# Retrieval by gathered rows for 160 of 512 tokens instead of 128, with 72 expert blocks computed ahead instead of 48

## The chip, the cores and the metric

The kernel runs on one core of one Trainium2 chip. A core has TensorE (matrix products; PE in the profile), VectorE (DVE), ScalarE (ACT), GpSimd (POOL) and SyncE (SP), which here only starts transfers. Each engine works through its own queue in order and waits at semaphores for the others. The metric is the time of one execution on the device in microseconds (us), the median of several runs.

## The reference

One decoder layer on 512 tokens of width 1024 in float32: gated linear attention and sliding-window attention, merged into x, and then product-key retrieval of single-neuron experts (PEER), which the change is about:

```
def peer_layer(xn, w_pq, sub_keys, expert_u, expert_v):
    qp = (xt @ w_pq).reshape(t, 8, 2, 128)
    scores = jnp.einsum('thpd,hpkd->thpk', qp, sub_keys)
    s_top, i_top = lax.top_k(scores, 16)
    ...
    best, pos = lax.top_k(cand, 16)
    idx = jnp.take_along_axis(cand_idx, pos, axis=-1)
    gate = jax.nn.softmax(best, axis=-1)
    ...
        u = expert_u[ib]
        h = jax.nn.gelu(jnp.einsum('lkd,ld->lk', u, xb), approximate=False)
        return jnp.einsum('lk,lkd->ld', gb * h, expert_v[ib])
```

Each token chooses 8 x 16 = 128 of 16384 experts, and an expert is one row of U and one row of V, 1024 wide.

## The kernel before

Attention, merging and the queries of the retrieval come first (up to 660 us); the change leaves them almost alone. The retrieval then treats the tokens in two ways.

*Dense tokens.* For 384 tokens (TD) all experts are computed. There are 128 blocks of 128 experts. A **U block** (`h_step`) multiplies a block of U with the normalised tokens: 8 x 3 = 24 matmuls with a moving operand of TD columns, since each float32 is split into a high part (`whi`, made by ScalarE) and a low part (`wlo`, made by VectorE, by GpSimd for the first blocks) and three of the four products are kept. Gelu by ScalarE puts the result into a ring of SBUF tiles. A **V step** (`v_step`) weights it with the gates (`wr`, then its parts `wh` and `wl`) and multiplies with a block of V: 3 groups of 128 tokens x 3 products x 2 halves of 512 columns = 18 matmuls, summed in PSUM over all 128 blocks. The stream `st` loads and splits the weights two blocks ahead, with three tiles each for raw, `whi` and `wlo`.

*The gates* of the dense tokens are sparse, and are made dense by one-hot products: `decode` finds the expert numbers of 128 tokens on VectorE, TensorE transposes them (`ijp`, read by ScalarE into `ijg`), `onehot` makes two one-hot matrices for 4 tokens on VectorE, `gmm` multiplies them on TensorE (`gp`), ScalarE copies the product into `gbuild`, and after every 8 groups of 4 tokens ScalarE's queue writes 2 MB of gates to DRAM (`gd`). Later `gt` reads them back by block.

*Gathered tokens.* For the other 128 tokens (TG), one to a partition, GpSimd gathers by indirect transfer one row of U for each of the 128 chosen experts, and VectorE multiplies it with the token and sums (L1128); then 128 rows of V, which VectorE adds up with their weights (L1131). That is 256 steps of 128 x 1024.

*Order.* All is written out by hand. N0 = 48 U blocks run ahead. The ring holds NRING = 32 results; the blocks between 32 and 48 are spilled to DRAM (`hs<-hw`, L1154, from ScalarE's queue) and read back later (`hr`). Between the pieces of these blocks `feed` puts steps of the generator `route`: decoding and the one-hot groups. Then `dense_order` mixes: a V step, and behind it one of the remaining U blocks where a ring tile is free (a **pair**), else the V step alone. Gather steps begin at block 47 and are dealt out by a fixed count (`work(0.7)`, `work(1.5)`):

```
    for n, (kind, b) in enumerate(todo):
        if kind == "U":
            h_step(b)
            work(1.5)
            continue
        paired = n + 1 < len(todo) and todo[n + 1][0] == "U"
        h_load(b + WA + 2)
        w_a(b + WA)
        work(0.7 if paired else 0.4)
        w_b(b + WA)
        v_step(b)
        work(0.7 if paired else 0.4)
```

Rows are gathered four at a time into one of two buffers (`gbuf`): the next four are asked for when the first of the current four is used.

Of the kernel before, what the change touches and what calls it, by code (L numbers as in the profile page):

```python
# [20 lines left out]
D = 1024  # L21
# [13 lines left out]
RS = (4, 6, 7)  # L35
DS = (4, 6, 8, 11, 13, 15, 18, 23)
# [8 lines left out]
N0 = 48  # L45
NRING = 32
NOO = 6
AHEAD = 5
LEAD = 11
TAIL = 3  # L50
GL = 2
GS = 1
WA = 2
TG = 128
# [25 lines left out]
def tile_block(ctx, tc, xT, wst, smalls, wgk2, keysT, uT, vv, u_rows, v_rows, out):  # L80
# [736 lines left out]
    xtok = XP.tile([128, D], F32, name="xtok")  # L817
    x1s = DR.tile([128, NT, D], F32, name="x1s")
# [111 lines left out]
    for hp in range(17):  # L930
        if hp < 16:
# [26 lines left out]
        if hp in (5, 6):  # L958
            xtok_fill(hp - 5)
        if hp == 7:  # L960
            c16 = XP.tile([128, 16, 128], BF, name="c16", tag="xn0")
            clo = XP.tile([128, 16, 128], BF, name="clo")
            for c_, steps in ((c16, ((0, 16, 1, 0),)), (clo, LO)):
                for a0, na, st_, b0 in steps:
                    nc.gpsimd.iota(c_[:, a0:a0 + na], pattern=[[st_, na], [0, 128]], base=b0, channel_multiplier=0,
                                   allow_small_or_imprecise_dtypes=True)
        if hp:
            scores(hp - 1)
        if hp % 2 and hp >= 3:
            cands((hp - 3) // 2)  # L970
# [5 lines left out]
    eidx = XP.tile([128, 128], I32, name="eidx")  # L976
    wgt = XP.tile([128, 128], F32, name="wgt")
# [14 lines left out]
    def positions():  # L992
# [5 lines left out]
        nc.vector.scalar_tensor_tensor(q, pf, 48.0, i3, OP.is_ge, OP.add)  # L998
        nc.vector.scalar_tensor_tensor(q2, q, 0.5, i1, OP.mult, OP.add)
# [4 lines left out]
    def eq_mult(t, sd):  # L1004
        eq = R.tile([128, 16, 128], BF, name="eq", tag="eq", bufs=1)
        nc.vector.tensor_tensor(eq, pb[:, sd, t, None, :].to_broadcast([128, 16, 128]), c16 if sd else clo,
                                OP.is_equal if sd else OP.is_ge)
        e4 = eq.rearrange("p a (k h) -> p a k h", h=8)
# [4 lines left out]
    def decode(t):  # L1013
# [48 lines left out]
    def route():  # L1062
# [7 lines left out]
        nc.vector.tensor_copy(kh(pbf[:, 0]), posu.rearrange("p t h k -> p t k h"))  # L1070
        positions()
# [3 lines left out]
        nc.scalar.activation(b32, b32, AF.Exp)  # L1075
        yield
        d1 = decode(1)
        for _ in range(7):
            next(d1)
        ss = R.tile([128, 32], F32, name="gsum")  # L1080
        nc.vector.tensor_reduce(ss, b32, AX.X, OP.add)
        nc.vector.reciprocal(ss, ss)
        nc.vector.tensor_tensor(b32, b32, ss[:, :, None].to_broadcast([128, 32, 16]), OP.mult)
        yield
        next(d1, None)
        n = 32 * (NT - 1)
        for i in range(AHEAD):
            onehot(i)
        yield
        dec = None  # L1090
        for i in range(n):
            if i % 32 == DS[0]:
                dec = decode((i // 32 + 2) % NT)
            if dec is not None and i % 32 in DS:
# [6 lines left out]
    def gather():
# [232 lines left out]
```

## Time and profile before

| | |
|---|---|
| median of 3 runs | 1855.3 us (1854.67 to 1855.85) |
| the profiled execution, its own time | 1860.8 us |
| its span, first to last instruction | 1859.0 us |
| mean granted TensorE clock | 0.99 of full speed |
| busy | TensorE 1799.7 us, VectorE 1336.0, ScalarE 746.4, GpSimd 590.5 |
| moved by transfers | 387.14 MB |

Busy time is the time in which an engine has an instruction under way. Matmuls overlap in the engine's pipeline, so a row's duration is longer than the distance from one matmul to the next; how long a block takes is read from the starts in the chain. Of TensorE's clock the profile gives the share of full speed that was granted.

### The profile page before, as it was taken

How to read it: one execution, taken by the hardware profiler on the slowest of the kernel's cores; microseconds unless marked ns; L12 is line 12 of the kernel's file. 1: busy time of each engine (PE TensorE's matmuls, PEld its weight loads, DVE VectorE, ACT ScalarE, POOL GpSimd, SP SyncE). 2: the span in 40 equal slices, each digit the busy share in tenths (PEclk: the TensorE clock that was granted, in tenths of full speed). 3: DMA queues.
4: the chain of work that ended last, by engine and by line, in shares of the span. 5: the costliest groups of instructions: out<-in, count | busy, mean ns of one | idle time of the engine just before them, and what ended most of it. 6: DMA issues, size and time to landing. Idle time of an engine off the chain costs nothing.

```text
span 1859.0 us, 25029 instructions
## 1 busy us (share of the span) xinstructions
PE 1799.7 (97%) x9331; PEld 1568.1 (84%) x9331; DVE 1336.0 (72%) x2688; ACT 746.4 (40%) x1126; POOL 590.5 (32%) x433
## 2 busy tenths in 40 slices
PE   7999999999998998899999999999999999999998
PEld 5676688887887898899988898988899998988887
DVE  7657714355349988898867878777778888888764
ACT  4435523334253244566553333333333333333332
POOL 2433344444545530000013333331335343343100
PEclk9999999999999999899999999999999999999999
DMA  4221122222333233555788988998889999898753
GB/s 162 69 67 46 57 91 80 80 71 89 119 125 120 69 114 109 168 177 166 212 278 318 336 327 327 336 343 328 318 320 346 331 325 344 314 340 322 265 187 135
DMA packets 149018, 387.14 MB, mean 208 GB/s; under 512 B 11280, under 2 KB 64656, under 8 KB 148512
## 3 DMA queue, kind: packets, MB, share of 16 engines
q1 hardware_dynamic: 60368, 223.00, 33.8%
q0 software_dynamic: 36864, 134.23, 20.2%
q10 hardware_dynamic: 51664, 28.31, 5.4%
q8 instruction: 73, 1.20, 0.3%
q14 instruction: 49, 0.40, 0.1%
HBM read 353.00 MB, written 32.51 MB: 207 GB/s over the span
## 4 chain that ended last, share of the span: by engine, by line
PE 51%; DMA 1%; ACTq 1%; ACT 0%; DVE 0%; issue 0%; DVEq 0%
PE hp L179 21%; PE oacc L1194 10%; PE oa__8345 L1194 5%; PE oa__8346 L1194 5%; PE oa__8347 L1194 5%; PE oa__8348 L1194 5%; PE gp L1055 2%; DMA hs<-hw 1%; ACTq L1154 1%; ACT gbuild L1056 0%; ACT hw L1152 0%; ACT whi L129 0%; DVE wlo L130 0%; ACTq L1060 0%; DVE oh L1044 0%
## 5 line engine op out<-in xcount | busy, mean ns | idle before, releaser
L129 ACT CAST whi<-raw 128x1024 fp32r<-128x1024 f32 x349 | 365.0, 1047 | 226.2 <-issue 87.3
L130 DVE TENSOR_TENSOR wlo<-raw,whi 128x1024 fp32r<-128x1024 f32 x252 | 308.7, 1225 | 153.5 <-ACT whi L129 153.2
L179 PE MATMUL hp<-xh,whi 128*128 128x384 f32 x1024 | 354.3, 346 | 3.6 <-ACT hw L1152 3.6
L179 PE MATMUL hp<-xh,wlo 128*128 128x384 f32 x1024 | 345.8, 338 | 5.5 <-DVE wlo L130 5.5
L179 PE MATMUL hp<-xl,whi 128*128 128x384 f32 x1024 | 345.9, 338 | 0.0
L1108 POOL DMA_INDIRECT rows<-in_u_rows_dram,eidx x128 | 144.2, 1126 | 543.2 <-DVE oh L1044 277.5
L130 POOL TENSOR_TENSOR wlo<-raw,whi 128x1024 fp32r<-128x1024 f32 x97 | 239.8, 2476 | 237.0 <-ACT whi L129 236.2
L1108 POOL DMA_INDIRECT rows<-in_v_rows_dram,eidx x128 | 147.4, 1151 | 231.3 <-DVE acc L1131 184.2
L179 PEld LDWEIGHTS hp<-xh,whi 128*128 128x128 f32 x1024 | 194.4, 190 | 7.5 <-ACT hw L1152 3.9
L179 PEld LDWEIGHTS hp<-xh,wlo 128*128 128x128 f32 x1024 | 194.1, 190 | 6.2 <-DVE wlo L130 6.2
L179 PEld LDWEIGHTS hp<-xl,whi 128*128 128x128 f32 x1024 | 194.6, 190 | 3.4
L1152 ACT ACTIVATE ring<-hp 128x384 f32<-128x384 f32 x112 | 55.7, 497 | 313.8 <-PE hp L179 312.9
L1131 DVE SCALAR_TENSOR_TENSOR acc<-rows,wgt,acc 128x1024 f32<-128x1024 f32 x128 | 163.9, 1280 | 0.7
L1128 DVE SCALAR_TENSOR_TENSOR rows<-rows,xtok 128x1024 f32<-128x1024 f32 x128 | 154.7, 1220 | 0.0
L1056 ACT COPY gbuild<-gp 128x512 f32<-128x512 f32 x96 | 105.9, 1123 | 60.9 <-PE gp L1055 60.2
L1184 DVE TENSOR_TENSOR wl<-wr,wh 128x384 fp32r<-128x384 f32 x128 | 71.5, 558 | 71.8 <-ACT wh L1176 71.8
L1176 ACT CAST wh<-wr 128x384 fp32r<-128x384 f32 x128 | 65.3, 510 | 134.1 <-PE oa__8348 L1194 78.6
L179 PE MATMUL mm<-hhi,whi 128*128 128x512 f32 x264 | 108.0, 409 | 0.9 <-DVE gb L577 0.9
L1044 DVE TENSOR_SCALAR oh<-iof,ijg 128x128 f32<-128x128 f32 x384 | 107.1, 346 | 0.0
L1055 PE MATMUL gp<-oh 128*128 128x128 f32 x768 | 102.9, 278 | 1.6 <-ACT gbuild L1056 1.6
L179 PE MATMUL mm<-hhi,wlo 128*128 128x512 f32 x264 | 104.2, 395 | 0.0
L179 PE MATMUL mm<-hlo,whi 128*128 128x512 f32 x264 | 103.8, 393 | 0.0
(560 smaller groups left out, 3574.9 us busy)
## 6 DMA issues: line engine op xcount, KB each, us to landing
raw<-in_uT_dram SPq DMA_DIRECT2D x128, 512.0 KB, 5.1
raw<-in_vv_dram SPq DMA_DIRECT2D x128, 512.0 KB, 5.5
raw<-in_wst_dram SPq DMA_DIRECT2D x93, 512.0 KB, 3.4
gt<-gd SPq DMA_DIRECT2D x32, 768.0 KB, 6.5
gd<-gbuild ACTq DMA_DIRECT2D x11, 2048.0 KB, 10.7
hs<-hw ACTq DMA_DIRECT2D x16, 192.0 KB, 4.4
hr<-hs SPq DMA_DIRECT2D x16, 192.0 KB, 5.9
xt<-in_xT_dram SPq DMA_DIRECT2D x8, 256.0 KB, 6.6
```

The lines of the kernel that those rows point to most:

```text
L129: nc.scalar.copy(hi, r)
L130: self.lo_eng(u).tensor_tensor(lo, r, hi.bitcast(F32), OP.subtract)
L179: nc.tensor.matmul(ps[:, :n], a[:, kb, :], b[:, kb, c0:c0 + n], start=(kb == 0 and i == 0), stop=(kb == KB - 1 and i == 2))
L1044: nc.vector.tensor_scalar(o[:, 1, k], iof, ijg[:, 0, t0 + k:t0 + k + 1], ijg[:, 2, t0 + k:t0 + k + 1], OP.is_equal, OP.mult)
L1055: nc.tensor.matmul(p[:, k], o[:, 0, k], o[:, 1, k], start=True, stop=True)
L1056: nc.scalar.copy(gbs[c].rearrange("p i t -> p t i")[:, q * 4:q * 4 + 4, :], p)
L1108: nc.gpsimd.indirect_dma_start(out=b_[:, i], out_offset=None, in_=rows, in_offset=bass.IndirectOffsetOnAxis(ap=eidx[:, 4 * g + i:4 * g + i ...
L1128: nc.vector.scalar_tensor_tensor(cur[:, i], cur[:, i], 1.0, xtok, OP.mult, OP.mult, accum_out=hd[:, s_:s_ + 1])
L1131: nc.vector.scalar_tensor_tensor(acc, cur[:, i], wgt[:, s_:s_ + 1], acc, OP.mult, OP.add)
L1176: nc.scalar.copy(hi, wr)
L1184: nc.vector.tensor_tensor(lo, wr, hi.bitcast(F32), OP.subtract)
L1194: nc.tensor.matmul(accs[2 * t + hf], a[:, ts], v_[:, hf * 512:(hf + 1) * 512], start=(b == 0 and i == 0), stop=(b == NB - 1 and i == 2))
```

## The change

160 tokens are gathered, 352 computed densely. The 32 new gathered tokens lie on 128 partitions as four copies: copy r has the slots 32 r to 32 r + 31, so that 32 more gathers of U and 32 of V serve them (steps "x" and "y"), and a matmul with a 0/1 matrix (`sel`) adds the four partial sums at the end. A U block has 352 columns instead of 384; a V step has still 18 matmuls, with a first weight of 96 columns. There are 88 one-hot groups instead of 96. 72 blocks run ahead instead of 48, and the ring has 25 tiles instead of 32, so that 47 blocks are spilled instead of 16. The routing is cut into smaller steps, which stand after blocks 4 to 19 (`RS`) and then between pieces of blocks 20 to 66. Gather steps begin at block 19; they are dealt out by two running totals, `dve` and `pe`, to which the program adds a fixed number of microseconds for each piece of work that it issues: `pump` issues steps as long as VectorE's total is less than 3 us ahead of TensorE's. In the order 56 pairs and 72 lone V steps follow the first block of V (before: 80 and 48).

```diff
-RS = (4, 6, 7)
-DS = (4, 6, 8, 11, 13, 15, 18, 23)
+RS = (4, 7, 8, 10, 11, 11, 12, 13, 13, 14, 15, 16, 17, 18, 19)
+POOLLO = 8
+DS = {32: (4, 6, 8, 11, 13, 15, 18, 23), 24: (1, 3, 5, 7, 9, 11, 13, 16)}
...
-N0 = 48
-NRING = 32
+N0 = 72
+NRING = 25
...
-LEAD = 11
-TAIL = 3
+LEAD = 20
+TAIL = 5
+SLACK = 3.0
...
-TG = 128
+XG = 32
+XR = 128 // XG
+TG = 128 + XG
+TB = 128 - XG
...
-        nc.scalar.copy(xn0[:, kb], hr.pop(kb)[:, 0:TG])
+        h = hr.pop(kb)
+        nc.scalar.copy(xn0[:, kb, 0:128], h[:, 0:128])
+        nc.scalar.copy(xn0[:, kb, 128:].rearrange("p (r t) -> p r t", t=XG),
+                       h[:, None, 128:TG].to_broadcast([128, XR, XG]))
...
         if hp == NXU - 1:
+            for hf in range(4):
+                xtok_fill((xtok, xtk2)[hf // 2], hf // 2 * 128, hf % 2)
...
-        nc.vector.tensor_tensor(eq, pb[:, sd, t, None, :].to_broadcast([128, 16, 128]), c16 if sd else clo,
+        nc.vector.tensor_tensor(e4, pk[:, None].to_broadcast([128, 16, 16, 8]),
+                                (c16 if sd else clo)[:, :, None, :].to_broadcast([128, 16, 16, 8]),
                                 OP.is_equal if sd else OP.is_ge)
...
-        yield
         gk = R.tile([128, 128], F32, name="gkh", tag="gkh")
         nc.vector.tensor_copy(gk.rearrange("p (k h) -> p k h", h=8), gf)
+        if t == 1:
+            e1 = R.tile([128, 128], I32, name="e1")
+            nc.vector.scalar_tensor_tensor(e1, ij[:, 0], 128.0, ij[:, 1], OP.mult, OP.add)
+            for r in range(XR):
+                rs = slice(r * XG, (r + 1) * XG)
+                nc.sync.dma_start(eid2[rs, :], e1[0:XG, rs])
+                nc.sync.dma_start(wgt2[rs, :], gk[0:XG, rs])
+        yield
         p = PS.tile([128, 3, 128], F32, name="ijp", tag="PT")
...
+        steps = ([("u", s_) for s_ in range(128)] + [("x", s_) for s_ in range(XG)]
+                 + [("v", s_) for s_ in range(128)] + [("y", s_) for s_ in range(XG)])
...
+            while n < min(len(steps), k + (5 if late[0] else 4)):
+                for _ in range(4 if late[0] else 1):
...
+            dve[0] += (1.31 if kind in "vy" else 1.2) * (1.2 if late[0] else 1)
+            yield
...
-        for t in range(TD // 128):
-            ts = slice(t * 128, t * 128 + 128)
+        for t in range(3):
+            ts = slice(max(128 * t - XG, 0), 128 * t + 128 - XG)
...
+    def pump(slack):
+        while side and dve[0] < pe[0] + slack:
+            step()
...
+        if b == RS[0]:
+            dve[0] = 27.0
+        for _ in range(RS.count(b)):
             next(r_)
+        if b == RS[-1]:
+            side.append(gather())
...
+        if b >= RS[-1]:
+            pump(SLACK)
...
+            h_load(b + WA + 3)
+            w_a(b + WA)
+            pump(SLACK)
+            w_b(b + WA)
+            v_step(b)
+        pump(SLACK)
...
+                ps = PS.tile([128, 512], F32, name="xo", tag=f"M{hf}")
+                nc.tensor.matmul(ps[0:XG, :], sel, acc2[0][:, c], start=True, stop=True)
```

The built programs show what this does to the engines' queues. First VectorE's queue at the end of the first decode. `eq` and `ij` are the decode's tiles, `gkh` its last, which TensorE transposes. Before:

```order
L1010 TENSOR_TENSOR eq<-eq,idf 128x2048
L981 TENSOR_TENSOR eq<-eq 128x8x128
L981 TENSOR_TENSOR eq<-eq 128x4x128
L981 TENSOR_TENSOR eq<-eq 128x2x128
L984 TENSOR_TENSOR ij<-eq 128x128
L1081 TENSOR_REDUCE gsum<-gate 128x32
L1082 RECIPROCAL gsum<-gsum 128x32
L1083 TENSOR_TENSOR gate<-gate,gsum 128x512
L130 TENSOR_TENSOR wlo_5749<-raw_5694,whi_5748 128x1024
L130 TENSOR_TENSOR wlo_5782<-raw_5746,whi_5781 128x1024
L130 TENSOR_TENSOR wlo_5815<-raw_5779,whi_5814 128x1024
L1026 COPY gkh<-gate 128x128
```

In the change the same steps, with a block's low part (`wlo`) after every few of them:

```order
L134 TENSOR_TENSOR wlo_5930<-raw_5889,whi_5929 128x1024
L994 TENSOR_TENSOR eq<-eq 128x8x128
L994 TENSOR_TENSOR eq<-eq 128x4x128
L134 TENSOR_TENSOR wlo_5965<-raw_5927,whi_5964 128x1024
L1113 TENSOR_REDUCE gsum<-gate 128x32
L1114 RECIPROCAL gsum<-gsum 128x32
L1115 TENSOR_TENSOR gate<-gate,gsum 128x512
L994 TENSOR_TENSOR eq<-eq 128x2x128
L997 TENSOR_TENSOR ij<-eq 128x128
L1041 COPY gkh<-gate 128x128
L1044 SCALAR_TENSOR_TENSOR e_6003<-ij 128x128
L134 TENSOR_TENSOR wlo_6016<-raw_5962,whi_6015 128x1024
```

Before, no low part stands within the decode, and three stand behind it ahead of `gkh`; in the change one stands after every two to seven steps.

The second place is VectorE's queue in the lone V steps, in which a step is one low part, one `wr`, one `wl` and gather steps. Before, with the rows of U:

```order
L130 TENSOR_TENSOR wlo_10627<-raw_10576,whi_10626 128x1024
L1173 TENSOR_TENSOR wr<-hr,gt 128x384
L1184 TENSOR_TENSOR wl<-wr,wh 128x384
L130 TENSOR_TENSOR wlo_10659<-raw_10624,whi_10658 128x1024
L1128 SCALAR_TENSOR_TENSOR rows,hd<-rows,xtok 128x1024
L1173 TENSOR_TENSOR wr<-hr,gt 128x384
L1184 TENSOR_TENSOR wl<-wr,wh 128x384
```

In the change, with the rows of U of the 32 new tokens (`xtk`):

```order
L134 TENSOR_TENSOR wlo_11070<-raw_11024,whi_11069 128x1024
L1176 SCALAR_TENSOR_TENSOR rows,misc<-rows,xtk_3905 128x1024
L1234 TENSOR_TENSOR wr<-hr,gt 128x352
L1246 TENSOR_TENSOR wl<-wr,wh 128x352
L134 TENSOR_TENSOR wlo_11110<-raw_11067,whi_11109 128x1024
L1176 SCALAR_TENSOR_TENSOR rows,misc<-rows,xtk_3905 128x1024 x2
L1234 TENSOR_TENSOR wr<-hr,gt 128x352
L1246 TENSOR_TENSOR wl<-wr,wh 128x352
```

Before, 11 u steps stand in these 14 lone steps, in the change one and two by turns; in pairs it is 2.9 steps before, and 3.3 (rows of U) or 3.0 (rows of V) in the change. In the change `wl` follows `wr` directly everywhere; before, a gather step stood between them in about half of the V steps.

## Rows read from the trace of the kernel before

**Rows 1.** The page, first part: busy time, share of the span, instructions.

```profile
PE 1799.7 (97%) x9331; PEld 1568.1 (84%) x9331; DVE 1336.0 (72%) x2688; ACT 746.4 (40%) x1126; POOL 590.5 (32%) x433
```

**Rows 2.** Windows: length, busy us by engine, granted clock, DMA share, GB/s.

```profile
core 0: us, PE busy (x) PEld busy (x) DVE busy (x) ACT busy (x) POOL busy (x), PEclk, DMA share, GB/s
660.50:980.00 319.50, 295.90 (x1933) 293.08 (x1931) 265.39 (x728) 177.34 (x204) 20.20 (x15) 0.97 0.59 179
700.00:800.00 100.00, 86.63 (x557) 85.68 (x555) 87.51 (x215) 49.95 (x56) 0.00 (x0) 0.91 0.46 137
980.00:1250.00 270.00, 270.00 (x1345) 243.46 (x1346) 218.15 (x317) 94.45 (x128) 100.50 (x90) 0.99 0.91 331
1225.00:1230.00 5.00, 5.00 (x24) 4.20 (x23) 3.53 (x6) 2.99 (x4) 3.84 (x4) 1.00 1.02 405
1230.00:1235.00 5.00, 5.00 (x28) 4.68 (x27) 4.40 (x7) 1.62 (x3) 0.26 (x1) 1.00 1.03 411
1310.00:1715.00 405.00, 405.00 (x2028) 365.24 (x2027) 333.19 (x358) 142.35 (x194) 162.13 (x140) 1.00 0.91 332
```

**Rows 3.** The chain that ended last: start, us, what. hp: U block.

```profile
865.23 1.56 PE hp L179 x9
866.80 0.89 PE gp L1055 x8
...
979.97 2.93 PE oacc L1194 x6
...
1321.50 4.19 PE hp L179 x24
1325.69 1.40 PE oacc L1194 x6
...
1329.88 1.24 PE hp L179 x7
```

**Rows 4.** Waits in 700 to 800, then 900 to 980: total, times, longest.

```profile
PE ijp L1029 <- DVE gkh L1026: 8.0, 1, 8.0
PE hp L179 <- DVE wlo L130: 5.3, 1, 5.3
...
PE hp L179 <- ACT hw L1152: 3.6, 1, 3.6
```

**Rows 5.** VectorE's timeline at five places: start, us, line, tiles.

```profile
696.43 1.22 DVE L1006 TENSOR_TENSOR eq<-pb,clo 128x2048 bf16<-128x2048 bf16 x1
...
705.02 0.68 DVE L1081 TENSOR_REDUCE gsum<-gate 128x32 f32<-128x512 f32 x1
...
715.62 0.69 DVE L1041 TENSOR_TENSOR oh<-iof,ijg 128x512 f32<-128x512 f32 x1 [5.21 <-ACT ijg L1031]
...
717.25 0.69 DVE L1041 TENSOR_TENSOR oh<-iof,ijg 128x512 f32<-128x512 f32 x1
...
1319.21 1.23 DVE L130 TENSOR_TENSOR wlo<-raw,whi 128x1024 fp32r<-128x1024 f32 x1 [0.39 <-ACT whi L129]
1320.35 1.22 DVE L1128 SCALAR_TENSOR_TENSOR rows<-rows,xtok 128x1024 f32<-128x1024 f32 x1
1321.49 0.09 DVE L1128 DVE_READ_ACCUMULATOR rows<-rows,xtok 128x1 f32 x1
...
1541.39 2.60 DVE L1131 SCALAR_TENSOR_TENSOR acc<-rows,wgt,acc 128x1024 f32<-128x1024 f32 x2
1543.91 0.55 DVE L1173 TENSOR_TENSOR wr<-ring,gt 128x384 f32<-128x384 f32 x1
1545.05 0.56 DVE L1184 TENSOR_TENSOR wl<-wr,wh 128x384 fp32r<-128x384 f32 x1 [0.58 <-ACT wh L1176]
```

**Rows 6.** The gathered rows' tile, last line: from issue to landing.

```profile
DMA to landing us min/median/max: 4.2/7.4/11.8
```

**Rows 7.** ScalarE's timeline, and the spilled tile: ns min/median/max.

```profile
884.01 5.46 ACTq L1154 DMA_DIRECT2D hs<-hw  x1
...
L1154 ACTq DMA_DIRECT2D hs<-hw x16: 326/332/7524, 878.5 to 978.5; - x16
```

**Rows 8.** TensorE's timeline in the query stage.

```profile
574.19 0.50 PE L179 MATMUL mm<-xh,wlo 128*128 128x512 f32 x1 [1.61 <-POOL wlo L130]
```

More of the change, by code (lines that the diff above doesn't have):

```diff
@@ L817, in tile_block @@
     xtok = XP.tile([128, D], F32, name="xtok")
+    xtk2 = XP.tile([128, D], F32, name="xtk2")
     x1s = DR.tile([128, NT, D], F32, name="x1s")
@@ L868, in tile_block @@
     nc.sync.dma_start(x1s, x1t)
-    xn0 = XP.tile([128, KB, TG], F32, name="xn0", tag="xn0")
+    xn0 = F.tile([128, KB, 256], F32, name="xn0", tag="gr")
     XN, XU = (xh, xl), (xuh, xul)
-    qpt = [xtok[:, i * T:(i + 1) * T] for i in range(2)]
+    misc = XP.tile([128, 512], F32, name="misc")
+    qpt = [xtk2[:, 0:T], xtk2[:, T:], misc[:, 0:T]]
     hr, qps = {}, {}
@@ L1075, in route @@
         nc.scalar.activation(b32, b32, AF.Exp)
+        nc.vector.tensor_copy(kh(pbf[:, 0]), posu.rearrange("p t h k -> p t k h"))
+        pos_ = positions()
+        next(pos_)
+        dve[0] += 4.5
+        yield
+        next(pos_, None)
+        dve[0] += 3.5
         yield
         d1 = decode(1)
-        for _ in range(7):
+        for c in (2.4, 0.9, 0.5, 2.7, 0.9, 0.5):
             next(d1)
+            dve[0] += c
+            yield
         ss = R.tile([128, 32], F32, name="gsum")
@@ L1083, in route @@
         nc.vector.tensor_tensor(b32, b32, ss[:, :, None].to_broadcast([128, 32, 16]), OP.mult)
+        next(d1)
+        dve[0] += 2.8
         yield
         next(d1, None)
-        n = 32 * (NT - 1)
         for i in range(AHEAD):
             onehot(i)
[L1089 to L1094, printed above, removed]
+            dve[0] += 1.62
+            yield
@@ L1095, in route @@
+        dec, first, size = None, 0, (128 - XG) // 4
+        for i in range(NGR):
+            if i == first + size:
+                first, size = i, 32
+            k, t = i - first, (TG + 4 * i) // 128 + 1
+            if t < NT and k in DS[size]:
+                if k == DS[size][0]:
+                    dec = decode(t)
                 next(dec, None)
-            if i + AHEAD < n:
+                dve[0] += 1.15
+            if i + AHEAD < NGR:
                 onehot(i + AHEAD)
+                dve[0] += 1.62
@@ L1098, in route @@
             gmm(i)
+            pe[0] += 0.896
             yield
[L1101 to L1133 removed]
@@ L1217, in tile_block @@
             Lt = ctx.enter_context(tc.tile_pool(name="late", bufs=1, side="right"))
-            side.append(gather())
+            late[0] = True
         if b == N0 - GL:
             g_load(0)
-        if b == N0 - GS:
-            step()
+        if b >= RS[-1]:
+            pump(SLACK)
     big = PS.tile([128, 2, 512], F32, name="oacc", tag="S2")
-    accs += [big[:, 0], big[:, 1]] + [PS.tile([128, 512], F32, name="oa_", tag=tg) for tg in ("PT", "O", "M2", "M3")]
-    for b in range(WA):
-        w_a(b)
-        w_b(b)
-    gacc, todo = 0.0, list(DENSE[N0:])
-    def work(g):
-        nonlocal gacc
-        gacc += g
-        while gacc >= 1:
-            gacc -= 1
-            step()
+    oa = [PS.tile([128, 512], F32, name="oa_", tag=tg) for tg in ("PT", "O", "M2", "M3")]
+    accs += [oa[0][0:TB, :], oa[1][0:TB, :], oa[2], oa[3], big[:, 0], big[:, 1]]
+    todo = list(DENSE[N0:])
     for n, (kind, b) in enumerate(todo):
```

168 lines of the change are left out of this document (97 added, 71 removed).

## The prediction

> **What bounds the kernel now.** I read the page's first part, then the windows, the chain, the waits and the VectorE timeline of the stretches that the change touches. TensorE is busy 97% of 1859 us, VectorE 72% [rows 1]. From 980 on TensorE never idles: 270.00 of 270 and 405.00 of 405 us, while VectorE has 81 and 82% and the transfers move 331 GB/s at a DMA share of 0.91 [rows 2]. The chain shows the same: there it is a U block of 4.19 us, a V step of 4.19, a U block again [rows 3]. Only the stretch in which blocks run ahead is different. It goes from the first block at 660.5 to the first V step at 980: TensorE is busy 295.9 of 319.5 us at a granted clock of 0.97; in 700 to 800 alone it misses 13.4 us and the clock is 0.91 [rows 2]. The waits name the reason: 8.0 us for the transposes of the first decode, 5.3 for a low part from VectorE, 3.6 for the spilled Gelu late in the stretch [rows 4].
>
> **The change, part by part.**
>
> *Narrower U blocks.* Of each block's 24 matmuls 384 columns become 352. 24 matmuls of 384 take 4.19 us and 18 of 512 also 4.19 [rows 3], so 0.175 and 0.233 each: in proportion to columns, nothing fixed. 352 gives 3.84 a block, and 128 x 0.35 = 44.7 us saved. No row has 352 columns, so I keep 40 as the lower bound. V steps do not shrink: their moving operand is the 512-wide V, and a first weight of 96 columns instead of 128 leaves the matmul count.
>
> *Eight fewer one-hot groups.* One takes 0.89 us of TensorE between two pieces of a block [rows 3]: 7.1 us saved.
>
> *Routing in small portions.* In the stretch ahead the work is 48 x 4.19 + 96 x 0.89 = 286.5 of 319.5 us: 33 lost to waits and to the slower clock behind them. The 8.0 us came because a whole decode (8.6 us on VectorE, from 696.43 to 705.02 [rows 5]) and three low parts stood ahead of gkh, with TensorE's transposes directly behind. Now these steps lie one to a block over blocks 7 to 15. VectorE's queue is late there: I count it some 27 us behind the first block at the start and add 19 of routing and 10 of low parts up to gkh, 56 us, while the transposes stand at the end of block 15, 16 x 3.84 = 61. So that wait goes, and the slower clock behind it. New is a tight budget: over the 48 units from 20 on VectorE has 48 low parts of 1.14, 86 one-hot groups of 1.63, three decodes of 8.6 and 38 gather steps of 1.20 [rows 5], 266 us, against 48 x 3.84 + 88 x 0.89 = 263 of TensorE. Low parts are made two blocks ahead, which covers 3 us. (The decode's compare reads a small constant by broadcast now; I price the decode as before, and if its two compares of some 1.2 us doubled, three decodes would put 7 us more on VectorE here.) Spills go from 16 to 47. A spill issued right behind a gd write held ScalarE's queue 5.46 us, where the median is 0.33 [rows 7]; with about eleven gd writes among the spills that happens some ten times instead of five. On SyncE's queue eight small copies of the 32 tokens' indices and gates wait for VectorE at block 14, and the weight loads queued behind them wait too; three raw tiles are loaded ahead, and VectorE is at 56 us where TensorE is at 58, so I cost this at nothing; without that cover it is VectorE's delay, up to a block of 3.84. GpSimd has only gathers from block 8 on, and behind them nothing is queued but further gathers. I keep 13 of the 33 us: 20 saved, between 3 (30 stay) and 30.
>
> *Ahead of it.* ScalarE makes twice the xn0 copies in the query stage and TensorE eight more transposes, just where it waits 1.61 us for a low part already [rows 8]: 3 us lost, 0 to 8. The selector's two matmuls at the end and those transposes: 2 us.
>
> *From the first V step on.* TensorE has 56 pairs of 8.03 and 72 lone V steps, 751 us. Before, it lost nothing here; now the cover is thin. Counting the program's order by the rows (low part 1.14, u step 1.20, two v steps 2.52, and 1.55 from wr to the end of wl, of which 0.58 is VectorE's wait for ScalarE's cast, since no gather step stands between them any more [rows 5]), VectorE has 206 of 209 us in the first 26 pairs, 198 of 189 in the 45 lone V steps, 226 of 237 in the later pairs, 110 of 113 at the end. Only the lone steps are over, by 9, less the lead of a block. The transfers: in the first pairs 138 loads and gathers of 0.524 MB and 5 MB of gates, 77 MB in 209 us or 370 GB/s; in the lone steps, with the spilled blocks read back, 72 MB in 189 or 383. Scaling 331 GB/s at 0.91 to a full share gives 364: 14 us too little; the best 5 us stretches, 405 and 411 at 1.02 and 1.03 [rows 2], would leave room. I take 12 us lost of 0 to 23 from these two.
>
> A third cost has a farther bound. The next four rows are asked for when the current four begin, so the first has four steps to land: 9.7 us in the first pairs (a step each 2.43 us), 11.6 to 12.5 in the lone steps, 10.7 in the later pairs. Landing takes 7.4 us in the median, 11.8 at most [rows 6]. If every late group took 11.8, VectorE would stand 22 x 2.1 + 6 x 0.2 + 22 x 1.1 = 71 us, 49 beyond its spare 22. That is the upper bound of this stretch.
>
> The rule that speaks against the change is in the Trainium skill, "DMA: Bandwidth & Descriptors", section Specifications: HBM gives one NeuronCore about 358 GB/s. By it the two dense stretches take 216 and 202 us, 21 over TensorE's time, and the sum below would end at 1810 instead of 1801. This trace does not agree: 405 and 411 GB/s over 5 us each [rows 2]; no row shows how long such a rate lasts.
>
> *Sum.* -44.7 - 7.1 - 20 + 3 + 2 + 12 = -54.8 us, made against the profiled execution's 1860.8 (span 1859.0): 1806.0. That execution lies 5.5 above the median of 1855.3, so 1801 for the median. By the bounds: -45 - 7 - 30 + 0 + 2 + 0 = -80, or 1775; -40 - 7 - 3 + 8 + 2 + 49 = +9, or 1864.
>
> **The rivals.**
>
> *The transfers set the pace* in the first pairs and the lone V steps, at 364 GB/s or less, and VectorE's 9 us come on top: 23 or more in place of 12, 1812, up to 1830 where queues lengthen the landings. For it: a share of 0.91 already now. Against: the 405 and 411. The skill's figure belongs here with its 1810.
>
> *The stretch ahead keeps its losses.* ScalarE's stalls come ten times, VectorE has 266 us of 263 and can't catch up, so all 33 us stay: 1821, and 1830 if the stalls reach TensorE at 3 us each. For it: both engines fuller than now. Against: around the stall at 884 TensorE kept working for most of it, since three banks of one-hot products and two of blocks stand between.
>
> *Everything hides.* The 12 in the V stretch and most of the 13 ahead go: 1775 to 1788. For it: 870 us of TensorE without a gap now, with VectorE in order behind it.
>
> *Rows come late: slower.* Landing grows with the load. With landing L in all late groups the loss is 22(L - 9.7) + 6(L - 11.6) + 22(L - 10.7) + 10(L - 12.5) - 22: it passes 67 us, where nothing is gained, at 12.2, and at 13 us it is 114, which makes 1903. For it: 7.4 at 331 GB/s, and four buffers' depth unchanged. Against: 11.8 is the longest of 256 now, and a late VectorE asks for less.
>
> **How the numbers follow.** Forecast, 1788 to 1812: 0.46. Transfers, 1812 to 1830 (the rule's 1810 counted in): 0.18. Losses ahead stay, 1821 to 1830: 0.13. All hides, 1775 to 1788: 0.10. Late rows: 0.13, of which 0.03 end within 0.2% of 1855.3, about what a measurement of this kernel can tell from no change, and 0.10 above. The predicted time is 1801. The range 1780 to 1836 leaves out the best part of the fourth case and the last. Faster 0.87, same 0.03, slower 0.10.
>
> **What would show it.** A U block in the chain at 3.84 us, V steps still 4.19. The first V step near 1030 (660.5 + 3 + 1 + 72 x 3.84 + 88 x 0.89 + 13 = 1032). No wait of TensorE for the first transposes; the granted clock above 0.97 in the stretch ahead. From there 751 us plus some 12 of waits, on low parts in the lone V steps above all; VectorE at 93% or more, GB/s near 375 in the first pairs. Wrong would be: a first V step beyond 1045 (losses ahead stay), waits of VectorE for rows in most groups of four, or TensorE waiting for low parts throughout the pairs.

## The result, and the profile after: 1.3% slower

The changed kernel took 1881.6 us in the median of four executions (1873.95 to 1884.43), the kernel before 1855.6 beside it (1854.67 to 1855.85): a ratio of 1.013, interval 1.0106 to 1.0155. The forecast was 1801, and the rival that ended on this side ("rows come late") isn't what happened. The profiled execution took 1882.7 us, span 1881.0. One execution of a run below (spill_on_sync, 2258.0 us at a granted clock of 0.72) is left out of its median, since all others had 0.98 or more.

The page of the change, first part, against [rows 1]:

```profile
PE 1780.0 (95%) x9279; PEld 1498.7 (80%) x9279; DVE 1391.0 (74%) x2746; ACT 729.2 (39%) x1129; POOL 722.5 (38%) x502
```

TensorE has 20 us less to do, and the span is 22 us longer: 42 us more in which it waits. The windows say where (columns as in [rows 2]): the stretch ahead, two places in it, the first pairs, the first lone V steps, the later pairs, the last lone V steps.

```profile
665.93:1070.44 404.51, 367.44 (x2444) 363.10 (x2443) 339.08 (x819) 197.60 (x242) 101.54 (x72) 0.97 0.73 246
780.00:980.00 200.00, 191.15 (x1337) 189.18 (x1336) 183.52 (x428) 112.99 (x135) 35.24 (x23) 0.99 0.80 261
1020.00:1060.00 40.00, 29.06 (x169) 28.09 (x169) 26.01 (x43) 14.56 (x18) 20.07 (x14) 0.87 0.95 339
1080.00:1250.00 170.00, 170.00 (x882) 150.33 (x881) 149.45 (x223) 61.60 (x84) 96.35 (x68) 1.00 0.97 363
1280.00:1490.00 210.00, 194.05 (x783) 135.21 (x782) 164.19 (x211) 60.72 (x85) 77.52 (x59) 1.00 0.90 332
1520.00:1700.00 180.00, 179.67 (x929) 157.91 (x928) 157.64 (x158) 62.66 (x90) 77.88 (x67) 1.00 0.95 352
1750.00:1860.00 110.00, 103.22 (x419) 72.69 (x419) 85.64 (x99) 33.03 (x46) 27.60 (x23) 1.00 0.77 271
```

In the pairs TensorE works without a gap, as before. Both stretches of lone V steps now have gaps, though VectorE is busy only 78% there, less than in the pairs; the first V step comes at 1070.4, forecast 1032. The chain that ended last shows a one-hot group and half a U block of the stretch ahead, then a U block of the pairs, then the turn of one lone V step (a row of the chain ends where the next one starts, so it can be shorter than the instruction):

```profile
863.19 0.89 PE gp L1080 x8
864.09 1.91 PE hp L183 x12
...
1206.44 3.99 PE hp L183 x24
...
1383.87 1.23 DVE wlo L134
1385.10 1.20 DVE accv L1188
1386.29 0.45 DVE wr L1234
...
1386.83 0.50 ACT wh L1238
...
1387.37 1.06 ACT whi L133
```

Where [rows 3] had U block, V step, U block, no TensorE stands in the chain of the lone steps at all. It is a circle of VectorE and ScalarE: low part, gather step, `wr`, ScalarE's cast `wh`, behind it in ScalarE's queue the cast `whi` of the next weights, and the next low part. VectorE's timeline of one such step, and the waits of 1280 to 1490 (total, times, longest):

```profile
1389.60 2.60 DVE L1188 SCALAR_TENSOR_TENSOR accv<-rows,misc,accv 128x1024 f32<-128x1024 f32 x2
1392.12 0.52 DVE L1234 TENSOR_TENSOR wr<-hr,gt 128x352 f32<-128x352 f32 x1
1393.26 0.53 DVE L1246 TENSOR_TENSOR wl<-wr,wh 128x352 fp32r<-128x352 f32 x1 [0.63 <-ACT wh L1238]
1394.21 1.22 DVE L134 TENSOR_TENSOR wlo<-raw,whi 128x1024 fp32r<-128x1024 f32 x1 [0.42 <-ACT whi L133]
```

```profile
ACT wh L1238 <- DVE wr L1234: 146.4, 42, 5.0
...
DVE wl L1246 <- ACT wh L1238: 23.5, 37, 0.9
...
DVE wlo L134 <- ACT whi L133: 18.2, 42, 0.7
```

VectorE waits twice in nearly every lone step, 0.63 and 0.42 us: together 41.7 of 210 us, nearly all of the 22% in which it isn't busy. ScalarE meanwhile waits 146 us for `wr`, although it could cast the next weights in that time: `whi` stands behind `wh` in its queue.

By stages, in us (starts of the first blocks from TensorE's timeline; a forecast row is the prediction's own price times the count, with 1 us for the selector):

| stage | forecast | measured | more |
|---|---|---|---|
| first U block starts | 664.5 | 665.9 | 1.4 |
| 72 U blocks and 88 groups, nothing lost | 354.8 | 356.0 (15 blocks of 4.00, 57 of 2 x 1.91, groups of 0.89) | 1.2 |
| lost in the stretch ahead | 13 | 48.5 | 35.5 |
| 25 pairs | 200.8 | 204.7 | 3.9 |
| 45 lone V steps and the next | 192.7 | 222.3 | 29.6 |
| 31 U blocks, 30 V steps | 244.7 | 250.4 | 5.7 |
| 27 lone V steps and the selector | 114.1 | 128.3 | 14.2 |
| allowed for losses from the first V step on | 12 | in the rows above | -12 |

So three rows hold nearly all of the miss: 35 us ahead, and 44 in the two rows of lone V steps, where 12 were allowed. (The last column adds up to 79.5 us and the span missed by 76.8: the kernel before took 874.3 us from its first V step to its last matmul where the same prices give 871.5.)

### The profile page after: what moved, and what is told of

Read it like the earlier page. It is cut to its first block, busy times and chain, and to the rows that moved or that the text cites. A ratio compares the mean times of both kernels' runs of the same rounds, so it can differ in the third digit from the quotient of the medians.

```text
span 1881.0 us, 25204 instructions
## 1 busy us (share of the span) xinstructions
PE 1780.0 (95%) x9279; PEld 1498.7 (80%) x9279; DVE 1391.0 (74%) x2746; ACT 729.2 (39%) x1129; POOL 722.5 (38%) x502
## 4 chain that ended last, share of the span: by engine, by line
PE 57%; DVE 21%; ACT 7%; issue 6%; DMA 5%; ACTq 2%; POOL 1%; SPq 1%; DVEq 0%; POOLq 0%
PE hp L183 18%; PE mm L183 16%; ACT whi L133 4%; PE mm L200 4%; PE oacc L1256 4%; DVE wlo L134 4%; DVE accv L1188 3%; PE gp L1080 3%; DVE rows L1176 2%; PE oa__9269 L1256 2%; PE oa__9271 L1256 2%; PE oa__9272 L1256 2%; PE oa__9270 L1256 2%; DVE accy L1188 2%; ACTq L1215 2%
## 5 line engine op out<-in xcount | busy, mean ns | idle before, releaser
L183 PE MATMUL hp<-xh,whi 128*128 128x352 f32 x1024 | 341.9, 334 | 11.1 <-ACT hw L1212 10.1
L183 PE MATMUL hp<-xh,wlo 128*128 128x352 f32 x1024 | 334.2, 326 | 14.9 <-DVE wlo L134 14.4
L134 POOL TENSOR_TENSOR wlo<-raw,whi 128x1024 fp32r<-128x1024 f32 x99 | 244.7, 2476 | 245.7 <-ACT whi L133 229.5
L183 PE MATMUL hp<-xl,whi 128*128 128x352 f32 x1024 | 333.1, 325 | 0.0
L1169 POOL DMA_INDIRECT rows<-in_v_rows_dram,misc x160 | 197.3, 1233 | 293.6 <-DVE accv L1188 172.8
L1238 ACT CAST wh<-wr 128x352 fp32r<-128x352 f32 x128 | 62.3, 487 | 448.3 <-DVE wr L1234 441.1
L1169 POOL DMA_INDIRECT rows<-in_u_rows_dram,misc x115 | 157.6, 1370 | 144.1 <-DVE rows L1176 101.2
L1169 POOL DMA_INDIRECT row<-in_u_rows_dram,misc x45 | 66.1, 1469 | 275.7 <-DVE row L1176 206.1
L1188 DVE SCALAR_TENSOR_TENSOR accv<-rows,misc,accv 128x1024 f32<-128x1024 f32 x128 | 164.1, 1282 | 2.1 <-DMA accv<-x1s 0.6
L1246 DVE TENSOR_TENSOR wl<-wr,wh 128x352 fp32r<-128x352 f32 x128 | 67.3, 526 | 76.2 <-ACT wh L1238 69.1
L1176 DVE SCALAR_TENSOR_TENSOR rows<-rows,xtok 128x1024 f32<-128x1024 f32 x83 | 99.0, 1221 | 5.4 <-DMA rows<-in_u_rows_dram,misc 5.3
```

Source lines behind the costliest of these rows:

```text
L134: self.lo_eng(u).tensor_tensor(lo, r, hi.bitcast(F32), OP.subtract)
L183: nc.tensor.matmul(ps[:, :n], a[:, kb, :], b[:, kb, c0:c0 + n], start=(kb == 0 and i == 0), stop=(kb == KB - 1 and i == 2))
L1169: nc.gpsimd.indirect_dma_start(out=rows[n], out_offset=None, in_=u_rows if kn in "ux" else v_rows, in_offset=bass.IndirectOffsetOnAxis(ap= ...
L1176: nc.vector.scalar_tensor_tensor(cur, cur, 1.0, x_, OP.mult, OP.mult, accum_out=h_[:, s_:s_ + 1])
L1188: nc.vector.scalar_tensor_tensor(acc, cur, w_[:, s_:s_ + 1], acc, OP.mult, OP.add)
L1246: nc.vector.tensor_tensor(lo, wr, hi.bitcast(F32), OP.subtract)
```

## Experiments: the lone V steps

Theory A: VectorE's two waits make the lone step. Rivals: B, VectorE has too many gather steps there; C, the transfers set the pace.

**weight_cast_first.** The split of a V step's weights is asked for ahead of `wr`, so that `whi` stands before `wh` on ScalarE:

```diff
             h_load(b + WA + 3)
+            w = get("V", b)
             w_a(b + WA)
             pump(SLACK)
             w_b(b + WA)
-            v_step(b)
+            v_step(b, w)
```

> The split of a V step's weights is asked for ahead of wr and wh, so that ScalarE's queue has whi before wh. Theory A (in a lone V step VectorE waits twice for ScalarE, 0.63 us for wh and 0.42 for whi, because whi stands behind a wh that waits for wr): the second wait goes, 72 x 0.42 = 30 us; 4.83 us per lone V step of the first lone stretch become 4.4, the whole some 1852 us (1845 to 1860), first V step unchanged near 1070. Rival B (VectorE has too many gather steps in the lone steps) and rival C (transfers set the pace): neither work nor bytes change, so 1874 to 1884.

Measured: 1871.7 us, ratio 1.009 (1.0072 to 1.0108). The last lone steps did what A says, 116.8 us in place of 128.3. The first ones became longer, 232.3 us in place of 222.3, 5.05 each. ScalarE's and SyncE's timelines there:

```profile
1390.07 1.05 ACT L133 CAST whi<-raw 128x1024 fp32r<-128x1024 f32 x1 [2.66 <-DMA raw<-in_vv_dram]
```

```profile
1386.84 0.32 SPq L1220 DMA_DIRECT2D hr<-hs  x1
1387.27 0.47 SPq L122 DMA_DIRECT2D raw<-in_vv_dram  x1
```

Now `whi` waits for its raw weights. Their load is issued right behind the read `hr` of a spilled block, in the moment in which `wr` (VectorE, 1386.30, 0.52 long) has emptied the buffer for it. Only the steps from the first stretch read spilled blocks; the last 27 don't, and there the edit worked.

**step_between.** The order is left as it is, and one gather step always stands between `wr` and `wl`:

```diff
             w_a(b + WA)
-            pump(SLACK)
+            step()
             w_b(b + WA)
```

> One gather step always stands between wr and wl; the rest is dealt out as before. Theory A: the step of 1.25 us covers both casts, wl and the low part wait no more, a lone V step takes TensorE's 4.19 us; 30 us come back in the 45 lone steps and 15 in the last 27: some 1838 us (1830 to 1848). Rivals B and C: VectorE has the same instructions and the transfers the same bytes, so 1874 to 1884.

Measured: 1832.5 us, ratio 0.9875 (0.9857 to 0.9894), faster than the kernel before. The first lone stretch took 194.1 us (4.22 a step), the last 115.2. VectorE's timeline:

```profile
1387.08 1.23 DVE L134 TENSOR_TENSOR wlo<-raw,whi 128x1024 fp32r<-128x1024 f32 x1
1388.22 0.52 DVE L1234 TENSOR_TENSOR wr<-hr,gt 128x352 f32<-128x352 f32 x1
1388.66 1.28 DVE L1188 SCALAR_TENSOR_TENSOR accv<-rows,misc,accv 128x1024 f32<-128x1024 f32 x1
1389.86 0.52 DVE L1246 TENSOR_TENSOR wl<-wr,wh 128x352 fp32r<-128x352 f32 x1
```

The same instructions, and in this step no `[... <-ACT]` behind `wl` or `wlo`. (In 1285 to 1455 `wl` never waits; `wlo` still waits 13 times, 15.0 us in all, but TensorE is busy 169.80 of 170.) A is shown, and B and C fall: VectorE's work and the bytes are those of the change, and the lone steps run at TensorE's pace. Of the 52.6 us between the two profiled executions, 28.2 + 13.1 = 41 lie in the two lone stretches. Most of the rest is a first V step 9 us earlier, which the edit doesn't touch: in the six kernels whose stretch ahead is that of the change (this one, the change, weight_cast_first, loads_before_spills, widths, uniform_widths) it comes anywhere from 1061.2 to 1070.4. Keep that scatter in mind in the next section, where each start of the first V step is read from one execution.

**loads_before_spills.** weight_cast_first, with the load of the next weights ahead of the read of a spilled block:

```diff
-            h_load(b + WA + 3)
             w = get("V", b)
+            h_load(b + WA + 3)
             w_a(b + WA)
```

> As weight_cast_first, and the load of the next weights is issued ahead of the read of a spilled block. Theory L: in weight_cast_first the load of raw stood on SyncE behind the read hr, which waits until wr has emptied its buffer; 0.4 + 6.7 (landing) + 1.05 (whi) + 1.2 (low part) + 0.5 (wr) and the hand-overs are 10 us for two lone steps, 5.0 a step where 4.97 was measured. With the load first a lone V step takes 4.4 us (VectorE's 3.8 and the 0.63 for wh that is left), the last 27 stay at 4.2, the whole is 1847 us (1840 to 1853). Rival C (the transfers themselves are too slow for the lone steps): 4.9 us a step as before, 1866 to 1876.

Measured: 1848.0 us, ratio 0.9945 (0.9929 to 0.9962). The lone steps took 202.7 us, 4.41 each, as forecast: one wait taken away, the one for `wh` left. C falls a second time.

## Experiments: the stretch ahead

The trace of the change shows three places. First, near 757 the pump issues the whole decode of the gathered tokens and two gather steps at once; each of the two waits for its rows, the second 1.22 us more. VectorE's timeline, then TensorE's:

```profile
757.62 0.26 DVE L1038 COPY misc<-gate 128x128 f32<-128x128 f32 x1
762.35 1.23 DVE L1176 SCALAR_TENSOR_TENSOR row<-row,xtok 128x1024 f32<-128x1024 f32 x1 [4.47 <-DMA row<-in_u_rows_dram,misc]
```

```profile
767.23 0.66 PE L183 MATMUL hp<-xh,wlo 128*128 128x352 f32 x1 [10.14 <-DVE wlo L134]
```

Second, ten times between 807 and 1033 a spill `hs` right behind a gate write `gd` holds ScalarE's queue, 2.6 to 16.1 us, and the weight casts queue behind it. Third, the end. ScalarE's timeline shows the longest of these stalls:

```profile
1031.10 0.92 ACTq L1085 DMA_DIRECT2D gd<-gbuild  x2
...
1032.56 16.12 ACTq L1215 DMA_DIRECT2D hs<-hw  x1
1048.78 1.04 ACT L133 CAST whi<-raw 128x1024 fp32r<-128x1024 f32 x1 [16.25 <-issue]
```

**spill_on_sync.** SyncE issues the spills:

```diff
         if NRING <= b < N0:
-            nc.scalar.dma_start(hs[b - NRING], g)
+            nc.sync.dma_start(hs[b - NRING], g)
```

> The writes of the spilled blocks are issued by SyncE, not ScalarE. Theory S (a spill issued behind a gate write holds ScalarE's queue 2.6 to 16.1 us, eleven times, and with it the weight casts): the stretch ahead loses some 18 us in place of 45, the first V step comes near 1045 in place of 1070, the whole some 1857 us (1850 to 1866). Rival T (the gate writes hold up the transfers themselves, whoever issues): the stalls show up on SyncE, weight loads come late, and the time stays 1874 to 1890; worse than that if SyncE, waiting for Gelu, holds the loads of each block.

Measured: 1876.0 us, ratio 1.010 (1.008 to 1.012). Half of theory S holds, and T falls: no spill holds SyncE for more than 0.57 us. From 780 to 980 nothing is lost any more:

```profile
780.00:980.00 200.00, 200.00 (x1423) 199.74 (x1422) 196.16 (x458) 117.24 (x139) 40.72 (x26) 1.00 0.85 277
```

That is 8.85 us more than in the change (the other five kernels with its stretch ahead lose 6.0 to 7.6 there), but the first V step comes only at 1059.5, where TensorE waits 15.61 us for it. GpSimd's and VectorE's timelines say why:

```profile
1042.86 0.93 POOL L1169 DMA_INDIRECT rows<-in_u_rows_dram,misc  x1 [14.52 <-DMA gd<-gbuild]
```

```profile
1051.33 1.23 DVE L1176 SCALAR_TENSOR_TENSOR rows<-rows,xtok 128x1024 f32<-128x1024 f32 x1 [11.26 <-DMA rows<-in_u_rows_dram,misc]
...
1058.43 0.52 DVE L1234 TENSOR_TENSOR wr<-ring,gt 128x352 f32<-128x352 f32 x1
```

Gates and gathered rows share two buffers. The last gate write (issued at 1017.9) holds one of them to 1042; the rows for it land at 1051; VectorE waits for them, with the first `wr` behind.

**first_rows_wait.** After the first rows are asked for, no gather step until the next block (`hold` is an empty list at the start):

```diff
-        while side and dve[0] < pe[0] + slack:
+        while side and not hold and dve[0] < pe[0] + slack:
             step()
+        hold.clear()
...
+            if k == 0:
+                hold.append(1)
+                yield
             cur = rows.pop(k)
```

> After the decode of the gathered tokens the first rows are asked for, and no gather step is issued until the next block. Theory D (10.1 us of TensorE near 757 are a decode of 9 us and then a VectorE that waits 5.7 us for rows just asked for, with the next low part behind): the wait shrinks to some 2 us, the first V step comes 8 us earlier, 1873 us or so. Rival: VectorE is late in all of this stretch and the next stall takes the 8 us back; first V step within 3 us of 1070.

Measured: 1877.6 us, ratio 1.0125 (1.0103 to 1.0146). My 2 us were wrong. The one wait became two, 1.97 and 6.74 us: the decode alone costs some 2, and the first row came 9.4 us after the decode's end (753.1 to 762.54), with one block's work of 3 us to cover it. One block isn't enough; four_edits puts three there, and TensorE's waits for low parts between 740 and 790 come to 5.3 us. The first V step came at 1063.1, where 8 us less was forecast, but that is within the scatter of 1061.2 to 1070.4 and shows nothing by itself.

**spill_on_sync_tail_9.** spill_on_sync, and the gate groups end nine blocks ahead of the first V step:

```diff
-TAIL = 5
+TAIL = 9
```

> As spill_on_sync, and the last gate groups come nine blocks ahead of the first V step in place of five. Theory G (at the end of the stretch the last gate write lands 24 us after its issue, the second row buffer is free only then, its rows land 8 us later, and VectorE waits for them with the first wr behind): the 15.6 us wait of the first V step goes, first V step near 1044 in place of 1059.5, the whole some 1862 us (1855 to 1868). Rival V (VectorE is the limit of the stretch ahead, 266 of 263 us, and has the routing in four blocks less): low parts come late and the first V step stays within 4 us of 1059.

Measured: 1878.0 us, ratio 1.0112 (1.0095 to 1.0129), first V step 1057.1. Theory G as I put it falls: the wait moved to where the buffers change hands. VectorE still waits 11.4 us for rows in 980 to 1057, TensorE 7.1 and 5.7 us for the low parts behind it. So it may be that the gates weren't late but the gather steps came too early, which the next run tries.

**spill_on_sync_one_step.** spill_on_sync, and after the last gate group one gather step a block:

```diff
         if b >= RS[-1]:
-            pump(SLACK)
+            if late[0]:
+                step()
+            else:
+                pump(SLACK)
```

> As spill_on_sync (gate groups five blocks ahead), and after the last gate group one gather step a block in place of as many as the budget gives. Theory R (the first V step waits because VectorE has run through the rows at hand, and stands, with wr queued behind, waiting for rows whose buffer the last gate write still reads): VectorE's 11.3 us wait goes, first V step from 1059.5 to 1046 to 1050, where the gates' own landing near 1042 and their reading back bound it; the steps put off fit into the pairs, where VectorE has 12% left; the whole 1866 us (1858 to 1872). Rival: the gates come late by themselves, first V step beyond 1055 and 1874 to 1880.

Measured: 1871.5 us, ratio 1.0076 (1.006 to 1.0091), first V step 1049.8 in place of 1059.5. Theory R holds for the place: VectorE's wait of 11.3 us is gone, and the first `wr` waits 4.3 us for the gates read back instead. Of the 10 us, 5 came back in the first pairs (210.2 in place of 205.1 us), which I had thought to be covered.

**four_edits, five_edits, five_edits_tail_5.** All together: step_between, spill_on_sync, TAIL 9 and three blocks without gather steps behind the first rows (`hold.extend([1] * 3)`, and `del hold[:1]` for `hold.clear()`); then one step a block as well; then with TAIL 5.

> step_between, spill_on_sync, the gate groups nine blocks ahead, and no gather step for three blocks after the first rows are asked for. If the losses ahead are the three that the trace shows (first rows 11 us, spills behind gate writes 14, the end 20), the first V step comes near 1035 and the whole is 1806 us (1798 to 1816). Rival V (VectorE sets the pace of the stretch ahead): first V step beyond 1045 and 1816 to 1830.

> As four_edits (gate groups nine blocks ahead), and after the last gate group one gather step a block. Theory R: the waits of 5.3, 8.5 and 5.6 us at the end of the stretch ahead go, first V step from 1052 to some 1036, the whole 1809 us (1801 to 1818). Rival: the steps put off make VectorE the limit of the pairs or the lone steps, and 1820 to 1826 stays.

> As five_edits with the gate groups five blocks ahead, as in the change. If the last gate write's landing (24 us after its issue) bounds the first V step, it comes some 8 to 12 us later than in five_edits, the whole 1819 us (1812 to 1826); if only the rows did, the two agree within 4 us.

Measured: 1824.4 (0.9823, 0.9806 to 0.9839), 1825.6 (0.983, 0.9817 to 0.9844) and 1817.1 us (0.9791, 0.9776 to 0.9806). The first V step came at 1052.4, 1042.6 and 1038.2. five_edits was a miss: its first V step is 10 us earlier, and all of it is lost at 1068, where TensorE waits 11.25 us for a low part. The gate write wasn't the limit either: TAIL 5 is the faster. VectorE's timeline shows what the early changeover costs: the budget makes up for the steps put off in one burst. In five_edits ten gather steps stand in a row from 1050.5 to 1067.0, 4.6 us of it waits for rows, with the low part behind them; in five_edits_tail_5 it is six (TensorE waits 4.37 us) and in spill_on_sync_one_step five (2.31 us). No run dealt them out more slowly. The best of all, 2.1% faster than the kernel before, loses 13.35 us of 373.16 in the stretch ahead and 5.3 in the windows behind it (stretch ahead, first pairs, lone V steps, later pairs):

```profile
665.00:1038.16 373.16, 359.81 (x2442) 357.59 (x2440) 332.91 (x804) 196.97 (x242) 98.13 (x66) 0.99 0.75 255
1050.00:1240.00 190.00, 185.63 (x948) 164.20 (x947) 166.86 (x253) 67.57 (x92) 102.93 (x81) 0.98 0.99 380
1255.00:1440.00 185.00, 184.09 (x790) 140.73 (x789) 162.18 (x215) 64.56 (x89) 65.76 (x61) 1.00 1.00 383
1460.00:1690.00 230.00, 230.00 (x1194) 203.67 (x1193) 197.95 (x203) 83.31 (x115) 101.48 (x87) 1.00 0.95 358
```

## Experiments: what 352 columns take

In the pairs of the change, blocks of 3.99 and 3.80 us stand side by side, 3.92 in the mean, where 3.84 was forecast. Three kernels, one execution each, give some blocks other widths; `n` and `c0` are the columns and the first token of a block. The cut shows this line for widths, uniform_widths (which takes `c0=T - n`) and widths_ahead; Gelu still fills 352 columns, repeating 32 of them where a block has fewer:

```diff
-        ps = proj(w, XN, n=TD, c0=TG, bank=bank, each=each)
+        n, c0 = ((352, 160), (352, 128), (320, 192), (384, 128))[b % 4 if b >= N0 else 0]
+        ps = proj(w, XN, n=n, c0=c0, bank=bank, each=each)
...
+        n = TD if b < N0 else 288 if b < 97 else 320
...
+        n, c0 = ((352, 160), (352, 128), (320, 192), (336, 176), (368, 144))[b // 3 if b < 15 else 0]
```

> U blocks from 72 on take by turns 352 columns from token 160 (as in the change), 352 from token 128, 320 from token 192, 384 from token 128; the outputs of those blocks are left wrong. A pace in proportion to columns gives 3.84, 3.84, 3.49 and 4.19 us a block. Theory W (below some 380 columns the weight loads, 0.188 us long and 0.167 apart in the slow blocks, set the pace): 4.0, 4.0, 3.8 to 4.0 and 4.19. Theory P (the place of the first column matters): 3.8 throughout from token 128, 3.8 and 4.0 mixed from 160, and 3.49 for 320.

> U blocks 72 to 96 have 288 columns, 97 to 127 have 320; the outputs of those blocks are left wrong. In proportion to columns 3.14 and 3.49 us a block. Theory H (a width that is no multiple of 64 loses in part of the blocks, as 352 does with 3.80 and 3.99): 320 always near 3.5, 288 by turns near 3.1 and 3.3 or more. Rival (blocks of one width behind each other fall into a slower step, whatever the width): both mix two lengths.

> The first fifteen U blocks, which follow each other with nothing between, have by threes 352 columns from token 160, 352 from token 128, 320, 336 and 368; the outputs of the last three groups and of the second are left wrong. In proportion (4.19 us for 384) a block takes 3.84, 3.84, 3.49, 3.67 and 4.02 us. Theory S (352 has a slower step of 0.1667 us a matmul of its own, wherever its columns lie): 4.0, 4.0, 3.5, 3.7 and 4.0. Theory N (blocks that follow each other without a V step between lose 0.16 us each, whatever the width): 4.0, 4.0, 3.65, 3.83 and 4.18. Theory P (the first column's place): 4.0 and then 3.84.

**widths**, by turns: 3.80, 3.86, 3.51 and 4.19 us: in proportion, and W falls. **widths_ahead**, by threes: 3.80, 3.84, 3.52, 3.68 and 4.00: in proportion too, so that S, N and P all fall. The slower step belongs to no width (see the last section). **uniform_widths** showed something else. Blocks of 288 columns took 3.19 us and of 320 mostly 3.52, but the pairs got hardly shorter: 200.6 us for the first 25 (204.7 with 352) and 251.3 for the later part (250.4). VectorE's timeline over one later pair:

```profile
1579.33 0.52 DVE L1236 TENSOR_TENSOR wr<-ring,gt 128x352 f32<-128x352 f32 x1
1580.40 0.53 DVE L1248 TENSOR_TENSOR wl<-wr,wh 128x352 fp32r<-128x352 f32 x1 [0.55 <-ACT wh L1240]
1581.35 1.22 DVE L134 TENSOR_TENSOR wlo<-raw,whi 128x1024 fp32r<-128x1024 f32 x1 [0.42 <-ACT whi L133]
1582.49 1.28 DVE L1188 SCALAR_TENSOR_TENSOR accv<-rows,misc,accv 128x1024 f32<-128x1024 f32 x1
1583.68 1.26 DVE L134 TENSOR_TENSOR wlo<-raw,whi 128x1024 fp32r<-128x1024 f32 x1
1584.87 2.59 DVE L1188 SCALAR_TENSOR_TENSOR accv<-rows,misc,accv 128x1024 f32<-128x1024 f32 x2
1587.37 0.52 DVE L1236 TENSOR_TENSOR wr<-ring,gt 128x352 f32<-128x352 f32 x1
```

From `wr` to `wr` 8.04 us, and VectorE stands still only in the same two waits. TensorE's pair of 352 columns takes 8.1: the pairs of the change were within 0.1 us of VectorE's circle, and a U block narrower still would have given nothing.

## Why the prediction was wrong, step by step

- **Narrower U blocks**, -44.7 forecast: about right. 24 us came ahead (72 x 4.19 less 277.7) and 15 in the pairs (56 x 0.27), together 39, just under the lower bound of 40. "In proportion to columns" holds only for the faster of two steps, 3.80 us, and not for 4.00 (last section). V steps stayed at 4.19.
- **One-hot groups**, -7.1: right; a group is 0.89 in the chain, as in [rows 3].
- **Ahead of the first block**, +3: 5.4 by the first block's start, within 0 to 8 (1.2 to 5.8 in the other kernels).
- **Routing waits, 13 of 33 kept**: failed, 48.5 us in place of 13. The wait for the first transposes went, as forecast, but I looked only for what the change takes away there. The stalls behind gate writes were counted rightly ("some ten times") and then left without a price of their own, since TensorE had ridden over the one at 884; the seven of them in 780 to 980 cost 8.85 us (spill_on_sync). Two were not foreseen at all: the decode of the gathered tokens with its first rows in one piece, some 11 us (a wait of 10.14, and matmuls 0.29 us apart behind it, elsewhere 0.16: the granted clock is 0.87 in 740 to 780), and the end, where a spill stalls for 16.1 us behind the last gate write, 20.8 us (the last 120 matmuls in 40.8 us, at 0.167 each 20.0). At the end, by spill_on_sync_one_step, what matters is how early a gather step is issued, ahead of rows that can't be there yet; at 757 the trace says the same, but first_rows_wait took only 1.4 of the 10.1 us away. So the rival "the stretch ahead keeps its losses" had the place right, but the 48.5 us are more than its 33, and ScalarE's stalls between 780 and 980, which it priced, are the smallest of the three places.
- **Lone V steps**, "VectorE has 198 of 189": this is the step that failed most. 198 is 4.40 us a step, and it held one wait, 0.58 for `wh`. The second, of the low part for `whi`, stood in the very row that I quoted (0.39 at 1319.21 in [rows 5]) and was left out. With 0.42, and 0.63 for 0.58, a step is 4.87; measured are 4.83. Before, the same circle fitted into TensorE's pace. In its first lone stretch, 15 steps of 4.20 us, TensorE had no gap, and VectorE was busy 47.4 us and waited 15.4 for the same two casts, 62.8 of 63.0 (part of that is no need of its own, since the cast `wh` waited 15.0 us for TensorE). The window and the waits of the kernel before:

```profile
1250.00:1313.00 63.00, 63.00 (x272) 50.70 (x271) 47.38 (x70) 22.74 (x32) 14.88 (x15) 1.00 0.86 315
```

```profile
DVE wl L1184 <- ACT wh L1176: 8.9, 11, 1.6
...
DVE wlo L130 <- ACT whi L129: 6.5, 13, 1.8
```

There were 12 gather steps in these 15, and in five of 14 one stood between `wr` and `wl`. The change put 1.4 gather steps of 1.25 us into each (59 to 43 low parts in 1280 to 1490) and none between. Neither alone makes the longer step: the kernel before had the waits, and step_between has as many gather steps as the change, 62 to 44 low parts in 1270 to 1460, one of them always between. With it 41 of the 44 us were gone.

- **The transfers**: not the limit. The change moved 363 GB/s for 170 us with TensorE at 170.00 of 170, and the best kernel 380 and 383 over 190 and 185 us. The rule of the Trainium skill ("DMA: Bandwidth & Descriptors", Specifications, about 358 GB/s for one NeuronCore) isn't borne out by these runs, in which one core runs alone.
- **Rows come late**, the slower rival: wrong in the V stretch. VectorE waited 5.3 us in all for the grouped rows. The time ended on that rival's side of the range for another reason.
- **The signs named beforehand** held in part: a first V step beyond 1045 did mean losses ahead. VectorE was busy 88% of the first pairs, where 93% or more was forecast, and the granted clock ahead stayed at 0.97. The waits for low parts were foretold for the lone steps, only not their size, nor that they come from ScalarE's order.

## What to carry to other kernels

Price a step of a loop by following it once round both engines' queues: every wait in the timeline's brackets belongs into the sum, and an engine that is 78% busy can set the pace when its idle time is all waiting for a partner that waits for it. When work is dealt out by a budget of busy time, say at each place where it lands what it covers (a step between two halves of a hand-over is worth 1 us of wait) and what it needs (rows asked for 9 us earlier); and see what the budget does after steps were held back (here it made them up in a burst of ten). An edit that cures one wait in a queue, as weight_cast_first, shows the next one in the queue that feeds it.

## What the runs showed of the hardware, unexpected

The same instructions on TensorE run at one of two steps. The first fifteen U blocks stand behind each other in all kernels of the change's width. In seven executions each took 3.80 us, in six, the profiled one of the change among them, 4.00, with the granted clock at 1.00 in both. TensorE's timeline of the change, then of step_between:

```profile
680.00 0.33 PE L183 MATMUL hp<-xh,whi 128*128 128x352 f32 x1
680.16 0.33 PE L183 MATMUL hp<-xl,whi 128*128 128x352 f32 x1
680.33 0.33 PE L183 MATMUL hp<-xh,wlo 128*128 128x352 f32 x1
```

```profile
679.95 0.32 PE L183 MATMUL hp<-xl,whi 128*128 128x352 f32 x1
680.11 0.32 PE L183 MATMUL hp<-xh,wlo 128*128 128x352 f32 x1
680.27 0.32 PE L183 MATMUL hp<-xh,whi 128*128 128x352 f32 x1
```

A matmul every 0.167 us here and every 0.158 there: 3 us for the fifteen blocks. In the pairs of one execution both occur, and in a pattern. Number the blocks of U and V in the order in which TensorE takes them; their weights lie by turns in three tiles. In the twelve kernels that have 352 columns there (all but uniform_widths and widths), all 216 U blocks with weights in one of the tiles took 3.80 us, and 399 of the 452 in the two others 4.00. Two things say that the tile alone doesn't decide it: the first fifteen blocks go through all three and don't change their step, and in widths, where blocks of other widths stand between, 13 of the 14 blocks of the change's form took 3.80, whatever their tile. So what stands around a block has a part in it; the cause stays open. The two steps may be one reason why the change's times spread over 10 us, which no run shows; those of the kernel before, over all its executions, spread over 7 (1853.9 to 1860.8).
